# All queries ahead of the attention: four heads packed per weight tile, kept in DRAM

## The chip, the core and the metric

The kernel runs on one core of a Trainium2 chip. The metric is the time of one execution on the device, in microseconds (us); of the kernel before, three timed runs gave 2964.47, 2965.61 and 2966.31. TensorE (PE) multiplies, VectorE (DVE) and ScalarE (ACT) read its results out of PSUM banks and work on tiles in SBUF, GpSimd (POOL) does a few copies, and SyncE (SP) issues nearly all transfers (DMAs).

## The reference, cut to what matters

The kernel computes one step of a two-layer decoder trunk for 1024 prompt tokens and 32 sample tokens (8 sequences of 4). The change lies in the second layer's mixer. Its queries and their use:

```python
def dilated_mixer(h, w_q, q_norm, w_o, pos, attend):
    B, L, _ = h.shape
    q = (h @ w_q).reshape(B, L, N_GROUPS, N_KV, Q_PER_KV, HEAD_DIM)   # 3 x 4 x 2 x 128
    q = rope_partial(rms_norm(q, q_norm), pos)                        # per head; rotary on 32 of 128
    outs, lses = [], []
    for g, (win, dil) in enumerate(DIL_GROUPS):                       # (128,1), (512,4), (2048,16)
        o, l = attend(q[:, :, g], win, dil)
        ...
    w = jax.nn.softmax(jnp.stack(lses), axis=0)
    o = jnp.sum(w[..., None] * jnp.stack(outs), axis=0)
    return o.reshape(B, L, N_QH_GROUP * HEAD_DIM).astype(h.dtype) @ w_o
```

Here `h` is the normalised residual stream (1024 wide). There are 24 query heads of 128: 8 slots (4 key/value heads times 2), each with three dilations. The prompt's attention runs over windows of 128 keys in classes of the token's number (1, 4, 16 steps apart); the sample tokens look into a cache of 1024 older keys and values. Per slot the three results are mixed by their softmax denominators.

## The kernel before, in words

Activations lie transposed: 128 features on the partitions, T = 1056 tokens (1024 prompt, 32 sample) along a row, worked on in three chunks of 352. Every large product is made of three single-pass products: a weight and an activation are each split into a rounded high part and a rest (`whi`/`wlo`, `XH`/`XL`), and `whi*XH + whi*XL + wlo*XH` are summed. A query head needs 8 feature tiles times 3 times 3 chunks = 72 matmuls of 352 columns.

The part that the change touches begins when `shared_kv` has issued its last product, and ends when the FFN that follows begins. It is staged so:

- `shared_kv` makes the four keys and values, writes them to `Kd` and `Vd` in DRAM, and splits the residual into `XH`/`XL`. Of its two wide PSUM pools one is given up ahead of the last value product (`hand_over`), and three one-bank buffers `mq` take its place.
- `Mixer.queries(s)` makes the three heads of slot s, one `wtile` of 512 KB weights each, through `proj` (L937). Each chunk goes through `qk_head`: scaled by the token's `rstd` (L829), squared (L831), split, summed over the 128 features by two matmuls with a matrix of ones into `p_n` (L800, L801), turned into a norm by Ln and Exp (L802, L803), applied (L805; L809 for the dilated heads, which are put into classes on the way), and rotated (L817 to L820; 32 partitions).
- `Mixer.attend(s)` makes the 8 score tiles of the near window (L973) and 8 double tiles of the dilated ones (L984), each taken out by DVE with mask and minimum (L966) and by ACT with Exp (L967). The weights that mix the three results go once through DRAM (`scr`, `scr2`, `cA`). The value half (`dilated`, `near_by`) scales the tiles on DVE, transposes them on PE, copies them on ACT (L1022, L1043), multiplies them with the values into `p_o`, and stores `o` to `Ad`.
- `Mixer.sample(h, half)` runs after every second slot, twice: five cache tiles `kk` (256 KB, two buffers) into `p_ss`, a softmax, five tiles `vv` into `p_os`.
- After slot 7 the first half of the output product (4 of 8 slots) runs through the same `proj`, 288 matmuls on `OH`/`OL`; they too stand at L937.

The program is written in this order (queries of slot s+1 behind the attention of slot s), and a scheduler then sorts each engine's instructions within what the buffers allow: on TensorE, matmuls of the next slot's queries stand between those of the attention. An engine works its list in order; each instruction can wait for others.

Of the kernel before, what the change touches and what calls it, by code (L numbers as in the profile page):

```python
# [8 lines left out]
F32 = mybir.dt.float32  # L9
# [9 lines left out]
NP, NS = 1024, 32  # L19
# [12 lines left out]
QB = 4  # L32
# [3 lines left out]
def yoco_step_kernel(  # L36
# [10 lines left out]
    raw_stack, mma_stack, mmb_stack, mq_stack = (ExitStack() for _ in range(4))  # L47
# [23 lines left out]

    def hand_over():
        mma_stack.close()
        mm.pools.pop(0)
        return psum("mq", mq_stack, bufs=3)

    def close_products():
        raws.pools.pop()
        raw_stack.close()
        mma_stack.close()  # L80
        mmb_stack.close()
# [47 lines left out]
    Vd = dr.tile([T, 512], F32, name="Vd")  # L129

# [85 lines left out]

    def like(t, s, ps):
        return t[:, s] if len(ps.shape) == 2 else t[:, s].rearrange("p (c n) -> p c n", c=3)
# [9 lines left out]
    def norm_done(ssq, n=D):  # L228
# [564 lines left out]
    def qk_head(chunks, g, tab, tp, dst, pre, late, classes=False, early=False):  # L793
# [4 lines left out]
        def finish(s, q, t, th, tl):  # L798
# [5 lines left out]
            if not classes:  # L804
                nc.vector.scalar_tensor_tensor(dst[:, s], q, g, t, op0=ALU.mult, op1=ALU.mult)  # L805
                return
            e = min(s.stop, NP) - s.start
            u = slice(s.start // 4, (s.start + e) // 4)
            nc.vector.scalar_tensor_tensor(  # L809
                dst[:, :NP].rearrange("p (r u) -> p u r", r=4)[:, u], q[:, :e].rearrange("p (u r) -> p u r", r=4), g,  # L810
                t[:, :e].rearrange("p (u r) -> p u r", r=4), op0=ALU.mult, op1=ALU.mult)
            if e < CW:
                nc.vector.scalar_tensor_tensor(dst[:, NP:], q[:, e:], g, t[:, e:], op0=ALU.mult, op1=ALU.mult)
# [29 lines left out]
    def shared_kv(X, ssq, tp):  # L843
        with tc.tile_pool(name="kvp", bufs=1) as kvp:
# [4 lines left out]
            norm_done(ssq)  # L849
# [29 lines left out]
        return mq  # L879

    def to_class(ap):
        return ap.rearrange("p (u r) -> p r u", r=4)

    class Mixer:
        def __init__(self, st, mq):
            def pool(name, bufs, **k):
                return st.enter_context(tc.tile_pool(name=name, bufs=bufs, **k))

            self.mq = mq
            self.po = sm.pools[1]
            self.sc = pool("sc", 2, space=PSUM, side="right")
            self.tr = pool("tr", 1, space=PSUM, side="right")
            p = self.pool = pool("mx", 1)
            self.mask_a = p.tile([128, 256], F32, name="mask_a")
            self.mask_b = p.tile([128, 768], F32, name="mask_b")
            self.mask_s = p.tile([128, 656], F32, name="mask_s")
            self.Qs = [p.tile([128, 8, 32], F32, name=f"Qs{h}") for h in range(4)]
            self.kn = p.tile([128, 4, 32], F32, name="kn")  # L900
            self.os = p.tile([128, 8, 8, 4], F32, name="os")
            self.tab = [rope_table(p, i) for i in range(2)]
            self.head(0)
            self.pre = ln_exp_set()
            for h in range(4):
                nc.gpsimd.memset(self.Qs[h], 0.0)

        def loads(self):
# [3 lines left out]
            for h in range(4):  # L912
                nc.sync.dma_start(self.kn[:, h], Kd[h][:, NP:])

        def head(self, h):

            cols = slice(h * 128, (h + 1) * 128)
# [419 lines left out]
```

## Time and profile before

| | us |
|---|---|
| timed runs, median of 3 | 2965.61 |
| profiled execution | 2967.59 |
| its span | 2965.8 |
| TensorE busy | 2909.5 (98%) |
| VectorE busy | 1845.1 (62%) |
| ScalarE busy | 1085.1 (37%) |
| the mixer, first query matmul to first FFN matmul | 1473.3 to 2069.0 |

The span is what the profile covers of the profiled execution; 1.8 us lie outside it. Busy time counts matmuls whose ends are modelled, so a busy TensorE is not one at its peak. The stretch of the change is a fifth of the span; the rest of the kernel is the same in both.

### The profile page before, as it was taken

To read this page: it belongs to the slowest core of one execution; us is meant where nothing else is said; L and a number is where in the kernel's file an instruction comes from. 1 tells how busy PE (TensorE), PEld (TensorE's weight loads), DVE (VectorE), ACT (ScalarE), POOL (GpSimd) and SP (SyncE) were. 2 spreads that over 40 slices of the span, in tenths; PEclk is the share of its full clock that TensorE was granted. 3 is DMA by queue.
4 is the path that set the end of the run, shared out by engine and by line. 5 is a ranking of instruction groups with operands and counts; after the bars stand their busy time and mean duration, and the time that the engine had idled before them with its cause. 6 is when DMAs were issued, how large, how long until landed. Compare 5 with 4: busy or idle time off the path is not lost.

```text
span 2965.8 us, 47230 instructions
## 1 busy us (share of the span) xinstructions
PE 2909.5 (98%) x19920; PEld 2762.0 (93%) x19920; DVE 1845.1 (62%) x2769; ACT 1085.1 (37%) x1761; POOL 19.9 (1%) x44
## 2 busy tenths in 40 slices
PE   8999999999999999999999999999999999999999
PEld 7889898899999999999988879788899999999999
DVE  6345455776766544467687778784676666654364
ACT  5233333522222221235455555552532222231141
POOL 0000000000000000000000000000000000000000
PEclk9999999999999999999999999999999999999999
DMA  3121234322222442132433141334422222262123
GB/s 129 59 74 51 74 140 142 119 80 80 81 72 87 171 129 74 41 127 102 132 91 107 59 122 44 115 107 134 167 79 73 87 72 80 76 237 75 50 77 110
DMA packets 133987, 291.06 MB, mean 98 GB/s; under 512 B 34160, under 2 KB 58736, under 8 KB 132752
## 3 DMA queue, kind: packets, MB, share of 16 engines
q1 hardware_dynamic: 133040, 287.72, 29.4%
q8 instruction: 157, 2.57, 0.4%
q14 instruction: 54, 0.44, 0.1%
q10 hardware_dynamic: 736, 0.33, 0.0%
HBM read 216.14 MB, written 71.86 MB: 97 GB/s over the span
## 4 chain that ended last, share of the span: by engine, by line
PE 88%; DVE 6%; DMA 3%; ACT 2%; issue 1%; SPq 0%; DVEq 0%; ACTq 0%
PE mm L271 38%; PE be L207 13%; PE ga L207 9%; PE al L207 8%; PE mm L937 6%; PE mm L671 2%; PE p_s L984 1%; PE p_o L1052 1%; PE mm L289 1%; DMA vv<-in_cv_dram 1%; DMA kk<-in_ck_dram 1%; DVE hs L817 1%; DVE q L809 1%; PE p_s L973 1%; DVE q L819 1%
## 5 line engine op out<-in xcount | busy, mean ns | idle before, releaser
L134 ACT CAST whi<-raw 128x1024 fp32r<-128x1024 f32 (+2 forms) x244 | 197.6, 810 | 789.3 <-PE mm L271 578.5
L135 DVE TENSOR_TENSOR wlo<-raw,whi 128x1024 fp32r<-128x1024 f32 (+2 forms) x244 | 224.6, 921 | 80.0 <-ACT whi L134 79.9
L764 DVE TENSOR_TENSOR X<-mm,X 128x1056 f32<-128x1056 f32 (+1 forms) x100 | 121.1, 1213 | 235.7 <-PE mm L271 235.5
L271 PE MATMUL mm<-XH,wlo 128*128 128x352 f32 x1104 | 245.3, 328 | 4.7 <-DVE wlo L135 4.7
L271 PE MATMUL mm<-XH,whi 128*128 128x352 f32 x1104 | 249.3, 331 | 0.2 <-ACT q_in L295 0.2
L271 PE MATMUL mm<-XL,whi 128*128 128x352 f32 x1104 | 247.3, 328 | 0.2 <-DVE XL L138 0.2
L134 ACT CAST hw<-S 128x512 fp32r<-128x512 f32 x176 | 108.8, 621 | 314.7 <-PE ga L207 181.8
L271 PE MATMUL mm<-GH,wlo 128*128 128x352 f32 x1038 | 223.6, 324 | 0.0
L271 PE MATMUL mm<-GL,whi 128*128 128x352 f32 x1038 | 223.6, 323 | 0.0
L271 PE MATMUL mm<-GH,whi 128*128 128x352 f32 x1038 | 223.3, 323 | 0.0
L207 PE MATMUL be<-Bh,hw 128*128 128x264 f32 x1056 | 216.6, 286 | 5.2 <-ACT hw L134 5.2
L207 PE MATMUL be<-Bl,hw 128*128 128x264 f32 x1056 | 215.8, 286 | 0.0
L207 PE MATMUL be<-Bh,lw 128*128 128x264 f32 x1056 | 214.9, 285 | 0.0
L271 PEld LDWEIGHTS mm<-XH,wlo 128*128 128x128 f32 x1104 | 189.0, 190 | 8.0 <-DVE wlo L135 5.3
L271 PEld LDWEIGHTS mm<-XH,whi 128*128 128x128 f32 x1104 | 188.6, 189 | 8.2 <-issue 3.1
L271 PEld LDWEIGHTS mm<-XL,whi 128*128 128x128 f32 x1104 | 190.2, 189 | 4.1 <-issue 1.3
L937 PE MATMUL mm<-XL,whi 128*128 128x352 f32 x576 | 193.7, 336 | 0.0
L937 PE MATMUL mm<-XH,whi 128*128 128x352 f32 x576 | 193.7, 336 | 0.0
L937 PE MATMUL mm<-XH,wlo 128*128 128x352 f32 x576 | 189.3, 329 | 0.0
L271 PEld LDWEIGHTS mm<-GL,whi 128*128 128x128 f32 x1038 | 177.0, 188 | 0.3 <-DVE GL L135 0.2
L271 PEld LDWEIGHTS mm<-GH,whi 128*128 128x128 f32 x1038 | 176.6, 188 | 0.0
L271 PEld LDWEIGHTS mm<-GH,wlo 128*128 128x128 f32 x1038 | 176.5, 189 | 0.0
(342 smaller groups left out, 6292.9 us busy)
## 6 DMA issues: line engine op xcount, KB each, us to landing
raw<-in_w_fi_dram SPq DMA_DIRECT2D x88, 512.0 KB, 3.5
Gd<-g SPq DMA_DIRECT2D x44, 528.0 KB, 2.7
gr<-Gd SPq DMA_DIRECT2D x44, 528.0 KB, 4.9
raw<-in_w_fo_dram SPq DMA_DIRECT2D x64, 256.0 KB, 2.7
raw<-in_w_a_dram SPq DMA_DIRECT2D x24, 512.0 KB, 3.5
raw<-in_w_q_dram SPq DMA_DIRECT2D x24, 512.0 KB, 3.7
kk<-in_ck_dram SPq DMA_DIRECT2D x40, 256.0 KB, 3.5
vv<-in_cv_dram SPq DMA_DIRECT2D x40, 256.0 KB, 2.9
```

Of the source, the lines that this page charges most:

```text
L134: nc.scalar.copy(hi, x)
L135: nc.vector.tensor_tensor(lo, x, hi.bitcast(F32), op=ALU.subtract)
L207: nc.tensor.matmul(ps[:, c, :HC], a[:, k, :], b[:, c * HC:(c + 1) * HC], start=(first and k == 0 and i == 0), stop=(k == len(xs) - 1 and i ...
L271: nc.tensor.matmul(ps[:, c, :CW], a[:, k, :], b[k][:, c * CW:(c + 1) * CW], start=(k == 0 and i == 0), stop=(k == n - 1 and i == 2),)
L289: nc.tensor.matmul(ps, a[:, k, :], b[k][:, s], start=(k == 0 and i == 0), stop=(k == n - 1 and i == 2))
L671: nc.tensor.matmul(ps[:, c, :CW], raw[:, 128 * k:128 * k + 128], ps_[k][:, c * CW:(c + 1) * CW], start=(k == 0), stop=(k == 1))
L764: nc.vector.tensor_tensor(like(X[m], s, p), p, like(X[m], s, p), op=ALU.add)
L809: nc.vector.scalar_tensor_tensor(dst[:, :NP].rearrange("p (r u) -> p u r", r=4)[:, u], q[:, :e].rearrange("p (u r) -> p u r", r=4), g, t[: ...
L817: nc.vector.stream_shuffle(t[32:64], dst[:32], [(a + 16) % 32 for a in range(32)])
L819: nc.vector.tensor_tensor(dst[:32], dst[:32], tab[:32], op=ALU.mult)
L937: nc.tensor.matmul(ps, a[:, k, :], b[k][:, s], start=(k == 0 and i == 0), stop=(k == n - 1 and i == 2))
L973: nc.tensor.matmul(ps[:, :n], q[0][:, j * 128:(j + 1) * 128], self.KA[:, k0:k0 + n], start=True, stop=True)
```

## The change

A new function `queries()` makes all 24 heads before any attention. It works through six groups (a dilation g and four of the eight slots, t4). A group loads four heads' weights (4 x 512 KB) into one tile `RR` and makes four products, each packing 32 features of four heads, with the wide PSUM pools of `shared_kv` kept for them. The four squares are summed in `S`, one pair of matmuls per chunk with a block matrix of ones (`block_r`) gives all four heads' norms, the rotary part (now 128 partitions of the first product) is done once per group, and the token's `rstd` is not applied, since the head norm divides it out: only its small constant is kept (`Ed`, from `norm_done`). `finish` multiplies and writes 16 pieces of 32 partitions to `Qd` in DRAM. It runs one product late, behind the first product of the next group in the program's text.

The attention then reads `Qd` (`load`, four buffers). `attend` is cut in two: `scores(s+1)` is issued ahead of `values_out(s)`, with twice the `pA` and `pB` buffers; the transposes use two PSUM banks in turn.

```diff
@@ norm_done(ssq, n=D, eps=None)
+            if eps is not None:
+                nc.vector.tensor_scalar(eps[:, s], p, 128 * EPS / n, 128 * EPS * EPS, op0=ALU.mult, op1=ALU.add)
...
@@ shared_kv
-            norm_done(ssq)
+            eps = tp.tile([128, T], F32, tag="s", name="eps", bufs=4)
+            norm_done(ssq, eps=eps)
+            nc.sync.dma_start(Ed, eps)
...
-                if h == 3:
-                    mq = hand_over()
...

+    def queries():
+        with tc.tile_pool(name="qp", bufs=1) as qp:
+            E = qp.tile([128, T], F32, name="E")
+            gq = qp.tile([128, 4], F32, name="gq")
+            heads = [slice(32 * a, 32 * a + 32) for a in range(4)]
+            for a in heads:
+                for b in range(4):
+                    nc.scalar.dma_start(gq[a, b:b + 1], gains[heads[b], G_Q:G_Q + 1])
+            nc.sync.dma_start(E, Ed)
+            zo = qp.tile([128, 128], F32, name="zo")
+            nc.gpsimd.memset(zo, 0.0)
+            for a in heads:
+                nc.gpsimd.memset(zo[a, a], 1.0)
+            block_r = qp.tile([128, 128], F32R, name="block_r")
+            nc.vector.tensor_copy(block_r, zo)
+            pre = ln_exp_set()
+            def qt(name, tag, bufs=1, dtype=F32):
+                return qp.tile([128, T], dtype, tag=tag, name=name, bufs=bufs)
+            def put(g, out, x, f):
+                if g == 0:
+                    f(v3(out), x)
+                    return
+                for c in range(3):
+                    e = min(CW, NP - c * CW)
+                    u = slice(c * CW // 4, (c * CW + e) // 4)
+                    f(by_class(out[:, :NP])[:, :, u], to_class(x[:, c, :e]))
+                    if e < CW:
+                        f(out[:, NP:], x[:, c, e:])
+            def finish(g, t4, hb, S):
+                th, tl, t = qt("th", "th", dtype=F32R), qt("tl", "tl", dtype=F32R), qt("t", "t")
+                split(th, tl, S)
+                for c in range(3):
+                    s = slice(c * CW, (c + 1) * CW)
+                    p = sm.tile([128, CW], F32, tag="sm", name="p_n")
+                    nc.tensor.matmul(p, block_r, th[:, s], start=True, stop=False)
+                    nc.tensor.matmul(p, block_r, tl[:, s], start=False, stop=True)
+                    nc.vector.tensor_tensor(t[:, s], p, E[:, s], op=ALU.add)
+                nc.scalar.activation(t, t, AF.Ln, scale=1.0 / 128)
+                if g:
+                    nc.scalar.activation(by_class(S[:, :NP]), to_class(t[:, :NP]), AF.Exp, scale=-0.5)
+                    nc.scalar.activation(S[:, NP:], t[:, NP:], AF.Exp, scale=-0.5)
+                else:
+                    nc.scalar.activation(S, t, AF.Exp, scale=-0.5)
+                for b in range(4):
+                    nc.vector.tensor_tensor(hb[b], hb[b], S, op=ALU.mult)
+                    for a in range(4):
+                        nc.sync.dma_start(Qd[3 * (4 * t4 + a) + g][heads[b]], hb[b][heads[a]])
+            late = None
+            table = None
+            for g, t4 in ((0, 0), (1, 0), (2, 0), (1, 1), (2, 1), (0, 1)):
+                if table != (g > 0):
+                    table = g > 0
+                    cos, sin = qt("cos", "cos"), qt("sin", "sin")
+                    for a in heads:
+                        nc.sync.dma_start(cos[a], c_rope[int(table)][0:32])
+                        nc.sync.dma_start(sin[a], c_rope[int(table)][32:64])
+                RR = qp.tile([128, 4, 8, 128], F32, tag="RR", name="RR")
+                for a in range(4):
+                    nc.sync.dma_start(RR[:, a].rearrange("p k m -> p (k m)"), w_q[3 * (4 * t4 + a) + g])
+                hb = []
+                for b in range(4):
+                    hi, lo = (wp.tile([128, 8, 128], F32R, tag=t, name=t) for t in ("whi", "wlo"))
+                    split(*(t[:].rearrange("p k (a c) -> p a k c", a=4) for t in (hi, lo)), RR[:, :, :, heads[b]])
+                    ps = proj((hi, lo), XH, XL)
+                    h = qt("hb", "hb", 6)
+                    if b == 0:
+                        S = qt("S", "S")
+                        with tc.issue_after(pre.ins):
+                            nc.scalar.activation(v3(S), ps, AF.Square)
+                    else:
+                        q = qt("sq", "sq")
+                        nc.scalar.activation(v3(q), ps, AF.Square)
+                        nc.vector.tensor_tensor(S, S, q, op=ALU.add)
+                    put(g, h, ps, lambda o, i: nc.scalar.activation(o, i, AF.Copy, scale=gq[:, b:b + 1]))
+                    if b == 0:
+                        x = qt("hs", "hs")
+                        nc.vector.stream_shuffle(x, h, [(a + 16) % 32 for a in range(32)])
+                        nc.vector.tensor_tensor(x, x, sin, op=ALU.mult)
+                        nc.vector.tensor_tensor(h, h, cos, op=ALU.mult)
+                        nc.vector.tensor_tensor(h, h, x, op=ALU.add)
+                        if late:
+                            finish(*late)
+                    hb.append(h)
+                late = g, t4, hb, S
+            finish(*late)
...

@@ Mixer
+        def load(self, s):
+            q = [self.a.tile([128, T], F32, tag="q", name="q", bufs=4) for _ in range(3)]
+            for g in range(3):
+                nc.sync.dma_start(q[g], Qd[3 * s + g])
...
-                t = pool.tile([128, 256], F32, tag="pA", name="pA", bufs=8)
+                t = pool.tile([128, 256], F32, tag="pA", name="pA", bufs=16)
...
-                    t = pool.tile([128, 2 * n], F32, tag=f"pB{h}", name="pB", bufs=4)
+                    t = pool.tile([128, 2 * n], F32, tag=f"pB{h}", name="pB", bufs=8)
...
-                p = tr.tile([128, 3, 128], F32, tag="tr", name="p_t")
+                p = tr.tile([128, 3, 128], F32, tag="sm" if tr.n % 2 else "tr", name="p_t")
...
@@ mixer
-            mx = Mixer(st, mq)
-            q = mx.queries(0)
-            mx.loads()
+            mx = Mixer(st)
+            queries()
+            xh_stack.close()
+            close_banks()
+            mx.start()
+            now = mx.scores(mx.load(0))
             for s in range(8):
-                if s and s % 2 == 0:
-                    mx.head(s // 2)
-                mx.attend(s, q)
+                after = None
+                if s < 7:
+                    if s % 2:
+                        mx.keys(s // 2 + 1)
+                    after = mx.scores(mx.load(s + 1))
+                mx.values_out(s, *now)
                 if s % 2:
+                    if s < 7:
+                        mx.values(s // 2 + 1)
                     for half in range(2):
                         mx.sample(s // 2, half)
-                if s < 7:
-                    q = mx.queries(s + 1)
-            xh_stack.close()
+                now = after
```

Three places of the new order matter. The first is SyncE's list behind the last value head, `rows` being that head's values turned to rows. Before:


```order
L874 DMA Vd<-rows 128x8x128
L875 DMA Vd<-rows 32x128
L874 DMA out_dram<-rows 128x8x128
L875 DMA out_dram<-rows 32x128
L260 DMA raw<-in_w_q_dram 128x1024
L839 DMA tab_13252<-in_c_rope_dram 64x1056
L839 DMA tab_13254<-in_c_rope_dram 64x1056
L919 DMA KA<-Kd_157 128x1024
```

And after; behind these rows stand three more pairs of `cos` and `sin` and then the four loads of `RR`:

```order
L872 DMA out_dram<-rows 128x8x128
L873 DMA out_dram<-rows 32x128
L984 DMA mask_a<-in_c_mask_a_dram 128x256
L985 DMA mask_b<-in_c_mask_b_dram 128x768
L986 DMA mask_s<-in_c_mask_s_dram 128x656
L988 DMA kn<-Kd_157 128x32
L988 DMA kn<-Kd_158 128x32
L988 DMA kn<-Kd_159 128x32
L988 DMA kn<-Kd_160 128x32
L1005 DMA KA<-Kd_157 128x1024
L889 DMA E<-Ed 128x1056
L940 DMA cos<-in_c_rope_dram 32x1056
```

The query weight that stood directly behind the last value rows is gone, as are two others among the earlier heads' rows; the first packed weights stand behind seventeen other loads.

The second place is TensorE's list where one set of norms is formed (`p_n`). Before, within a slot's queries, with what each row waits for:

```order
L937 MATMUL mm<-XL_13211,whi 128x352
L801 MATMUL p_n<-htl,ones_r 128x352 [waits DVE_49]
L937 MATMUL mm<-XH_13203,wlo 128x352
L937 MATMUL mm<-XH_13204,whi 128x352
L937 MATMUL mm<-XL_13212,whi 128x352
L937 MATMUL mm<-XH_13204,wlo 128x352
L937 MATMUL mm<-XH_13197,whi 128x352
L800 MATMUL p_n<-hth,ones_r 128x352 [waits Activation_49]
L801 MATMUL p_n<-htl,ones_r 128x352 [waits DVE_49]
L937 MATMUL mm<-XL_13205,whi 128x352
```

After, at the end of the second group (the next begins with `mm<-XH_13223,whi`); the ends of the fourth and fifth read alike, those of the first and third have their `p_n` one product later:

```order
L278 MATMUL mm<-XL_13238,whi 128x352 x3
L278 MATMUL mm<-XH_13230,wlo 128x352 x3
L919 MATMUL p_n<-th,block_r 128x352 [waits Activation_49]
L919 MATMUL p_n<-th,block_r 128x352
L920 MATMUL p_n<-tl,block_r 128x352 [waits DVE_49]
L920 MATMUL p_n<-tl,block_r 128x352
L919 MATMUL p_n<-th,block_r 128x352 [waits DVE_49]
L920 MATMUL p_n<-tl,block_r 128x352
L278 MATMUL mm<-XH_13223,whi 128x352 [waits PE_49,Activation_49]
L278 MATMUL mm<-XH_13223,whi 128x352 x2
L278 MATMUL mm<-XL_13231,whi 128x352 x3
```

The matmuls of the norm stood between query matmuls, and now stand behind the group's last product and ahead of the next group's first.

The third place is TensorE's list at a sample half, where `kk` is the cache of keys. Before:

```order
L937 MATMUL mm<-XH_13199,whi 128x352
L937 MATMUL mm<-XL_13207,whi 128x352
L1083 MATMUL p_ss<-kk,Qs_13246 32x128 [waits DMAHW3_49]
L1083 MATMUL p_ss<-kk,Qs_13246 32x128 x3
L937 MATMUL mm<-XH_13199,wlo 128x352
L937 MATMUL mm<-XH_13200,whi 128x352
L937 MATMUL mm<-XL_13208,whi 128x352
L1083 MATMUL p_ss<-kk,Qs_13246 32x128 [waits DMAHW4_49]
L1083 MATMUL p_ss<-kk,Qs_13246 32x128 x3
L937 MATMUL mm<-XH_13200,wlo 128x352
L937 MATMUL mm<-XH_13201,whi 128x352
```

And after, with the transposes (`p_ts`) of the same half behind it:

```order
L1167 MATMUL p_ss<-kk,Qs_13265 32x128 [waits DMAHW2_49]
L1167 MATMUL p_ss<-kk,Qs_13265 32x128 x3
L1167 MATMUL p_ss<-kk,Qs_13265 32x128 [waits DMAHW6_49]
L1167 MATMUL p_ss<-kk,Qs_13265 32x128 x3
L1170 MATMUL p_ss<-kn,Qs_13265 32x16 x4
L1167 MATMUL p_ss<-kk,Qs_13265 32x128 [waits DMAHW7_49,DVE_49]
L1167 MATMUL p_ss<-kk,Qs_13265 32x128 x3
L1167 MATMUL p_ss<-kk,Qs_13265 32x128 [waits DMAHW0_49]
L1167 MATMUL p_ss<-kk,Qs_13265 32x128 x3
L1167 MATMUL p_ss<-kk,Qs_13265 32x128 [waits DMAHW1_49]
L1167 MATMUL p_ss<-kk,Qs_13265 32x128 x3
L1199 MATMUL p_ts<-ident,es 128x128 [waits DVE_49]
```

Between the cache tiles stood query matmuls, which wait for no transfer; now one cache tile's matmuls follow the other's.

## Rows read from the trace of the kernel before

**Rows 1.** The page: busy time and share of each engine

```profile
PE 2909.5 (98%) x19920; PEld 2762.0 (93%) x19920; DVE 1845.1 (62%) x2769; ACT 1085.1 (37%) x1761; POOL 19.9 (1%) x44
```

**Rows 2.** Stretches of the mixer: start:end, length, busy time of each engine, granted clock, DMA

```profile
1473.30:1976.60 503.30, 484.40 (x3308) 432.27 (x3308) 387.97 (x938) 272.00 (x652) 15.81 (x30) 1.00 0.29 85
1976.60:2069.00 92.40, 84.29 (x610) 71.57 (x609) 55.96 (x153) 36.46 (x81) 1.39 (x2) 0.96 0.56 175
1516.00:1651.00 135.00, 129.39 (x903) 114.37 (x904) 103.35 (x263) 71.98 (x179) 4.08 (x7) 0.99 0.29 83
```

**Rows 3.** Query products: minimum, median, maximum ns; first and last start

```profile
L937 PEld LDWEIGHTS mm<-XH,whi x576: 186/188/289, 1473.3 to 1976.0; 128*128 128x128 f32 x192
```

**Rows 4.** The chain that ended last, one pair of slots: start, length, what

```profile
1516.08 1.13 PE p_s L973 x4
...
1530.56 1.31 PE p_s L984 x8
1532.67 1.31 PE p_s L984 x8
...
1540.16 4.71 DMA scr<-stW
1544.88 2.27 DMA cA<-scr
...
1556.90 3.87 PE mm L937 x24
```

**Rows 5.** The same chain, the fourth pair

```profile
1919.16 0.98 PE p_s L973 x4
```

**Rows 6.** The same chain, the last slot and the output product

```profile
1989.38 2.72 PE mm L937 x8
...
2008.40 4.39 DMA kk<-in_ck_dram
...
2013.24 0.48 PE p_t L1020 x3
...
2021.97 1.98 PE p_o L1052 x16
...
2045.49 23.54 PE mm L937 x146
2069.03 3.07 PE mm L271 x19
```

**Rows 7.** SyncE's queue behind the last value head

```profile
1478.76 1.12 SPq L874 DMA_DIRECT2D out_dram<-rows  x1
...
1480.68 1.04 SPq L260 DMA_DIRECT2D raw<-in_w_q_dram  x1
1483.61 1.14 SPq L839 DMA_DIRECT2D tab<-in_c_rope_dram  x2
```

**Rows 8.** The chain at that place, and the stretch behind it

```profile
1479.93 3.56 DMA out_dram<-rows
...
1483.50:1493.50 10.00, 8.92 (x52) 8.10 (x52) 6.85 (x10) 6.16 (x12) 3.23 (x5) 1.00 1.03 281
```

**Rows 9.** ScalarE and VectorE on whole rows of 1056, and a strided copy

```profile
1473.17 1.18 ACT L137 ACTIVATE XH<-X,gt 128x1056 fp32r<-128x1056 f32 x1 [0.27 <-PE mm L271]
...
1475.66 1.06 ACT L134 CAST whi<-raw 128x1024 fp32r<-128x1024 f32 x1
...
1474.17 1.25 DVE L298 TENSOR_TENSOR vh<-mm,rstd 128x1056 f32<-128x1056 f32 x1
...
L1030 ACT COPY o<-p_o 128x512 f32<-128x512 f32 x4 | 4.3, 1082 | 0.5 <-PE p_o L1028 0.4
```

**Rows 10.** The granted clock around a wait of TensorE

```profile
1986.00:1988.00 2.00, 0.73 (x3) 0.45 (x3) 1.99 (x2) 0.70 (x1) 0.00 (x0) 1.00 1.10 144
...
1990.00:1992.00 2.00, 2.00 (x9) 2.00 (x8) 1.66 (x2) 0.00 (x0) 1.18 (x1) 0.50 0.69 201
2010.00:2020.00 10.00, 8.91 (x67) 6.73 (x67) 4.19 (x20) 5.26 (x10) 0.00 (x0) 1.00 0.43 105
```

More of the change, by code (lines that the diff above doesn't have):

```diff
@@ L31 @@
 EP_AT = (3, 5, 6)
-QB = 4
 @with_exitstack
@@ L46, in yoco_step_kernel @@
     xh_stack = ExitStack()
-    raw_stack, mma_stack, mmb_stack, mq_stack = (ExitStack() for _ in range(4))
+    raw_stack, mma_stack, mmb_stack = (ExitStack() for _ in range(3))
     def psum(name, stack=ctx, **k):
@@ L129, in yoco_step_kernel @@
     Vd = dr.tile([T, 512], F32, name="Vd")
+    Qd = [dr.tile([128, T], F32, name=f"Qd{k}") for k in range(24)]
+    Ed = dr.tile([128, T], F32, name="Ed")
     def split(hi, lo, x, g=None):
@@ L803, in finish @@
             nc.scalar.activation(t, t, AF.Exp, scale=-0.5)
[L804 to L813, printed above, removed]
+            nc.vector.scalar_tensor_tensor(dst[:, s], q, g, t, op0=ALU.mult, op1=ALU.mult)
         def rotate():
@@ new lines, in yoco_step_kernel, with __init__ @@
+    class Mixer:
+        def __init__(self, st):
+            self.st = st
+            a = self.a = self.open("mxa")
+            self.mask_a = a.tile([128, 256], F32, name="mask_a")
+            self.mask_b = a.tile([128, 768], F32, name="mask_b")
+            self.mask_s = a.tile([128, 656], F32, name="mask_s")
+            self.Qs = [a.tile([128, 8, 32], F32, name=f"Qs{h}") for h in range(4)]
+            self.kn = a.tile([128, 4, 32], F32, name="kn")
+            self.os = a.tile([128, 8, 8, 4], F32, name="os")
@@ L913, in loads, with open, start, keys @@
                 nc.sync.dma_start(self.kn[:, h], Kd[h][:, NP:])
-        def head(self, h):
+            self.keys(0)
+        def open(self, name, bufs=1, **k):
+            return self.st.enter_context(tc.tile_pool(name=name, bufs=bufs, **k))
+        def start(self):
+            self.mq = self.open("mq", 3, space=PSUM)
+            self.po = sm.pools[1]
+            self.sc = self.open("sc", 2, space=PSUM, side="right")
+            self.tr = Turns(sm.pools[0], self.open("tr", 1, space=PSUM, side="right"))
+            self.pool = self.open("mx")
+            self.values(0)
+        def keys(self, h):
+            self.KA = self.a.tile([128, NP], F32, tag="KA", name="KA")
+            nc.sync.dma_start(self.KA, Kd[h][:, :NP])
+            self.KB = self.a.tile([128, NP], F32, tag="KB", name="KB")
+            nc.gpsimd.tensor_copy(by_class(self.KB[:]), to_class(self.KA[:]))
+        def values(self, h):
             cols = slice(h * 128, (h + 1) * 128)
-            self.KA = self.pool.tile([128, NP], F32, tag="KA", name="KA")
-            nc.sync.dma_start(self.KA, Kd[h][:, :NP])
-            self.KB = self.pool.tile([128, NP], F32, tag="KB", name="KB")
-            nc.gpsimd.tensor_copy(self.KB[:].rearrange("p (r u) -> p r u", r=4), to_class(self.KA[:]))
             self.VB = self.pool.tile([128, 8, 128], F32, tag="VB", name="VB")
@@ L938, in proj, with scores @@
                 yield c, ps
[L940 to L943 removed]
+        def load(self, s):
+            q = [self.a.tile([128, T], F32, tag="q", name="q", bufs=4) for _ in range(3)]
+            for g in range(3):
+                nc.sync.dma_start(q[g], Qd[3 * s + g])
                 nc.gpsimd.tensor_copy(
                     self.Qs[s // 2][:, :, g * 8 + s % 2 * 4:g * 8 + s % 2 * 4 + 4],
[L946 to L958 removed]
+                    q[g][:, NP:].rearrange("p (b t) -> p b t", t=4))
+            return q
+        def scores(self, q):
+            pool, sc = self.pool, self.sc
             stA = pool.tile([128, 8, 2], F32, tag="stA", name="stA", bufs=2)
@@ L1191, in yoco_step_kernel @@
     sb.close()
-    mq = shared_kv(X, ssq, tp)
+    shared_kv(X, ssq, tp)
     sx.close()
-    close_products()
-    xp, op, X = mixer(mq)
+    close_raw()
+    xp, op, X = mixer()
     bg2 = sx.enter_context(tc.tile_pool(name="bg2", bufs=20, side="right"))
```

69 lines of the change are left out of this document (19 added, 50 removed).

## The prediction

> **What bounds the kernel now.** I read the page first: TensorE is busy 98% of the span, VectorE 62%, ScalarE 37% [rows 1]. A change that takes work from VectorE and ScalarE alone gains nothing while that holds, so the question is whether it holds in the mixer. The windows say yes for its first 503.3 us: TensorE works 484.4 of them at a granted clock of 1.00, and only 18.9 us are idle; in a pair of slots it works 129.4 of 135 us while VectorE works 103.4 [rows 2]. Only the last 92.4 us, where the queries have run out, are looser, at a granted clock of 0.96 [rows 2]. The chain of waits then shows what a query costs: 24 of its matmuls in 3.87 us, 0.161 us each [rows 4], so a head of 72 takes 11.6 us and the 24 heads (576 times three matmuls, [rows 3]) 278.2 us. The whole mixer, from the first query weights at 1473.3 [rows 3] to the first FFN matmul at 2069.0 [rows 6], takes 595.7 us. This is the stretch that I forecast; the rest is the same code.
>
> The first pair of slots begins at 1516.08 and the fourth at 1919.16 [rows 4, 5], so a pair takes 134.4 us. Of that, six heads are 69.6, and their 36 norm matmuls, as wide, are 5.8. So 59.0 us a pair is what attention and samples cost TensorE today, with their waits filled by query matmuls. That number decides the case, since the change takes the filler away.
>
> **The change, part by part.**
>
> *Query products.* Packing four heads' quarters changes which columns stand in a weight tile, not their number: 24 products of 72 matmuls stay, 278.2 us. The norm's matmuls fall from 144 to 36: 5.8 us, a gain of 17.4.
>
> *VectorE and ScalarE work.* Scaling by rstd goes, as do 24 separate rotations; they lay beside the products, in 103.4 of 135 us [rows 2]. Worth nothing on the path.
>
> *Start.* The packed weights come behind seventeen other loads in SyncE's queue, and the first of these waits until the value rows have landed (the pools reuse memory). Before, a query weight was issued at 1480.68 and the tables at 1483.61 [rows 7], right as the rows' transfer ended (1479.93 + 3.56 = 1483.49, [rows 8]); TensorE had two weights already loaded and stayed 8.92 of 10 us busy [rows 8]. Now nothing is at hand. The loads are 0.84 MB of masks, 0.06 of new keys, 0.52 of `KA`, 0.54 of `E`, 1.08 of tables and 2.1 of weights, 5.1 MB; at the 281 GB/s of that stretch [rows 8] 18.3 us, so 1501.8. The rounded weights take another 1.06 [rows 9]: TensorE starts near 1502.9, 29.6 us after 1473.3, of which the transposes of the last value head fill one: 28. If the transfers run at twice that speed it is 20, if SyncE's issues are the limit 34. Behind such an idle stretch the clock falls: the granted clock was 0.50 soon after a stretch with 0.73 of 2 us at work, and eight matmuls took 2.72 us where 1.29 were due [rows 6, 10]. I add 3 us, seen as a stretch of some 6 us at half speed. Together **31**.
>
> *Group ends.* For the second, fourth and fifth group the order has the norm's matmuls directly behind the group's fourth product and ahead of the next first one. TensorE then waits for the fourth product's square (1.18) and its store in classes on ScalarE, which is strided (1.08 for 512 columns, so 2.2 for 1056), the rounded sum (1.1) and its rest on VectorE (1.25), all from [rows 9], then six matmuls of 0.161 and one addition between banks (0.5): 7.3 us, three times, **22**. Below, nothing, if the sum is faster than the store; above, 30. The first and third groups have a product between, which hides it.
>
> *Hand-over.* The first attention tile reuses the memory of the query buffers, so it waits until the last sixteen pieces have landed. Behind the last product: square, addition, rounding and rest (4.7), norms (1.5), Ln and Exp (2.4), four multiplications (5.0) from [rows 9], four issues behind the last (1.6) and a landing (3.6, as [rows 8]): 18.8, and a first score tile, **20** (14 to 26). Nothing stands on TensorE's list there but six score matmuls.
>
> *Attention alone.* The order interleaves scores of a slot with values of the one before, so the round trip through `scr` is covered; but the sample's cache tiles now stand one behind the other, and each wait for `kk` (4.39 us, [rows 6]) is TensorE's own. The lower bound: sixteen score tiles at 2.11 us for four ([rows 4], 1530.56 to 1532.67) are 8.4, and the last slot's values took 10.7 from first transpose to last product ([rows 6], 2013.24 to 2023.95). A slot is 19.1, a pair 38.2, with about 6 for the two sample halves 44. The upper one: nothing is gained or lost against today, 59.0, and with cold matmuls more. Without filler the engines wait for each other at each tile (two score banks, VectorE's list in order), yet those waits are partly in the 59.0 already. I take 59.0, the measured one: four pairs less the 9 of the last pair's samples, which fall into the output product, 227, and 4 for matmuls at the lower clock, **231**.
>
> *Output product.* From the last `p_o` (2021.97 + 1.98) to the FFN took 45.1 us [rows 6] with 231 of the 288 matmuls; now 240 stand there: **46**.
>
> Sum: 31 + 278 + 6 + 22 + 20 + 231 + 46 = 634 us against 595.7, 38.3 more. The profiled execution would be 2967.6 + 38.3 = 3005.9 (span 2965.8, 1.8 outside); on the median of the runs, 2965.6 + 38.3 = **3004**.
>
> **A rule against the change.** The trace shows TensorE's clock at 0.50 after a wait that left it 0.73 of 2 us busy, and at 1.00 where it was busy 8.91 of 10 with small matmuls [rows 10]. The Trainium skill ("TensorE: Matmul & The Clock Gate", section "Loop structure matters more than you think") says that matmuls which follow one another keep the array at speed, while a loop that waits for a transfer ahead of its matmuls runs at the lower clock throughout. By that rule the sample blocks would pull the whole attention down; this case's rows bear it out at 1990 and speak against it at 2010. It is the second rival.
>
> **The rivals.**
>
> *1. Faster: the attention packs.* With no query matmul in between, scores and values run at the lower bound, 44 a pair: 4 x 44 - 6 = 170 instead of 231, 573 in all: 2943. For it: VectorE and ScalarE have far less to do, and the round trip is covered. Against it: `kk` waits, two score banks, and 71 us of new idle time that must first be paid. The point of decision: 192 us for the attention, 50 a pair.
>
> *2. Slower: the attention runs at half clock.* A matmul cost 2.72 / 8 = 0.34 at 0.50 against 0.161 [rows 6], 2.1 times. Most of the 44 us a pair are TensorE's; doubled, 80 a pair, 4 x 80 - 11 = 309, 78 more than the forecast: 3082. Decided by whether the waits at score and sample tiles come often enough to keep the clock down.
>
> *3. The start is covered:* if the pools let the weights load while the value rows are still written, the gap shrinks to 10 and the time to 2983. The list of SyncE speaks against it.
>
> *4. The change doesn't do what it says:* if scores and values don't overlap on the chip, a slot pays the round trip through DRAM (4.71 + 2.27 = 7 us, [rows 4]) and the pair is 73: 4 x 14 = 56 more, 3060. TensorE's list has them mixed, so this goes with rival 2.
>
> **How the numbers follow.** Forecast 0.55 (2985 to 3025); rival 1 0.17; rivals 2 and 4 0.16; rival 3 0.12. A measurement of this kernel can tell about 0.2%, 6 us, from no change. Rival 1 gives faster 0.17; no difference lies between it and rival 3, and takes 0.06 from the low ends of rival 3 and the forecast; the rest, 0.77, is slower. The range must leave out 0.2 at most: below 2950 lies most of rival 1, above 3065 most of rival 2, so **2950 to 3065**.
>
> **What would show it.** In the profile after: TensorE idle from about 1476 to 1503 with the weights' transfer as releaser; 24 products of 11.6 us; three gaps of 7 us in front of `p_n`; 20 us without matmuls behind the last product; then four pairs of 59 us at a granted clock of 0.9 or more, and 46 us of output product. Wrong it would be if a pair takes under 50 us, if the clock of the attention is near 0.5, or if the start gap is missing.

## The result

The changed kernel takes 3050.39 us (median of four runs, 3047.67 to 3053.27) against 2965.04 of the kernel before in the same session: a ratio of 1.0289 (95% interval 1.0271 to 1.0307), 85 us slower. The forecast was 3004, 38 us slower, with a range of 2950 to 3065. The sign and most of the mechanism held, the size did not: 47 us more than forecast were lost, 39 of them in one term of the sum.

The page of the changed kernel, its busy times (before: [rows 1]):

```profile
PE 2906.4 (95%) x19812; PEld 2763.3 (91%) x19812; DVE 1712.2 (56%) x2517; ACT 1035.2 (34%) x1591; POOL 18.5 (1%) x49
```

VectorE lost 133 us of work and ScalarE 50, and the kernel became slower: TensorE's work stayed (2906 against 2909 us) and its idle time grew. The windows, cut at the stages of the forecast; the columns are those of [rows 2]:

```profile
1472.50:1504.70 32.20, 1.64 (x12) 0.97 (x10) 3.45 (x5) 4.61 (x7) 3.67 (x10) 0.55 0.66 194
1504.70:1816.10 311.40, 297.29 (x1760) 292.68 (x1761) 116.79 (x112) 97.92 (x138) 1.21 (x4) 0.95 0.27 84
1816.10:1837.50 21.40, 3.16 (x11) 1.56 (x9) 9.80 (x13) 5.40 (x6) 0.00 (x0) 0.61 0.85 274
1837.50:2107.90 270.40, 217.50 (x1664) 168.57 (x1668) 158.52 (x660) 141.77 (x397) 10.84 (x23) 0.90 0.58 158
2107.90:2155.10 47.20, 47.16 (x369) 42.28 (x369) 22.15 (x48) 10.39 (x18) 0.00 (x0) 1.00 0.53 171
```

They are the start without weights, the six groups of products, the hand-over, the attention, and the output product up to the FFN's first matmul. Together 682.6 us, where before 595.7 lay between the same points (1473.3 to 2069.0, [rows 3, 6]); the last value product ended 0.8 us earlier. Beside the forecast:

| stage | forecast | measured |
|---|---|---|
| start, with the lower clock behind it | 31 | 32.2, and 2.5 for the first 18 matmuls |
| products, norms, group ends | 278 + 6 + 22 = 306 | 308.9 |
| hand-over | 20 | 21.4 |
| attention | 231 | 270.4 |
| output product | 46 | 47.2 |
| sum | 634 | 682.6 |

Four stages are right within 4 us. The attention is 39 us too long. What TensorE waited for there, and what it waited for in the pairs of slots before (first group: changed kernel, 1837.5 to 2108; second: kernel before, 1516 to 1976; total us, times, longest):

```profile
PE p_ss L1167 <- DMA kk<-in_ck_dram: 23.7, 13, 3.8
PE p_s L1054 <- DVE stA L1047: 16.5, 2, 14.3
PE p_os L1211 <- DMA vv<-in_cv_dram: 10.1, 7, 2.5
PE p_o L1136 <- ACT o L1114: 4.6, 6, 2.3
```

```profile
PE p_os L1127 <- DMA vv<-in_cv_dram: 5.1, 5, 1.8
PE p_t L1041 <- DVE pA L1038: 3.3, 3, 1.4
PE p_ss L1083 <- DMA kk<-in_ck_dram: 3.0, 4, 0.9
```

The waits for the cache tiles rose from 8.1 to 33.8 us; up to the FFN's first matmul they are 9.5 in the kernel before and still 33.8 in the changed one. (The 14.3 us at `stA` are the end of the hand-over, put down to the attention's first tile.) One sample block in the chain of waits, and the window over it:

```profile
1894.75 5.37 DMA kk<-in_ck_dram
1900.17 0.70 PE p_ss L1167 x8
1900.88 3.97 DMA kk<-in_ck_dram
1904.90 0.66 PE p_ss L1167 x8
1905.63 0.67 PE p_ss L1167 x8
1906.32 2.62 DMA kk<-in_ck_dram
1908.98 0.66 PE p_ss L1167 x8
```

```profile
1898.00:1908.00 10.00, 2.69 (x40) 1.23 (x40) 3.72 (x19) 1.12 (x3) 0.00 (x0) 0.56 0.77 222
1908.00:1918.00 10.00, 8.82 (x91) 5.35 (x92) 4.99 (x28) 4.27 (x16) 0.00 (x0) 0.76 0.60 197
```

A cache tile is four matmuls, and each stands as two instructions in the trace, so x8 is one tile. Two tiles, a wait for the next transfer, two tiles, a wait: TensorE works 2.69 of 10 us, its granted clock is 0.56 there, and 0.76 in the ten that follow, though it is busy again. A tile's eight instructions, which took 0.35 to 0.43 us before, now take 0.66.

### The profile page after: what moved, and what is told of

The parts are those of the page before. It is cut to its first block, busy times and chain, and to the rows that moved or that the text cites. A ratio compares the mean times of both kernels' runs of the same rounds, so it can differ in the third digit from the quotient of the medians.

```text
span 3049.8 us, 46799 instructions
## 1 busy us (share of the span) xinstructions
PE 2906.4 (95%) x19812; PEld 2763.3 (91%) x19812; DVE 1712.2 (56%) x2517; ACT 1035.2 (34%) x1591; POOL 18.5 (1%) x49
## 4 chain that ended last, share of the span: by engine, by line
PE 89%; DMA 4%; DVE 3%; ACT 2%; issue 1%; SPq 0%; ACTq 0%; DVEq 0%
PE mm L278 46%; PE be L204 13%; PE ga L204 8%; PE al L204 8%; PE mm L678 2%; PE mm L1026 2%; DMA kk<-in_ck_dram 1%; DMA vv<-in_cv_dram 1%; PE p_s L1054 1%; PE mm L296 1%; PE p_o L1136 1%; PE p_s L1065 1%; PE p_u L506 1%; PE p_us L524 1%; PE p_o L515 1%
## 5 line engine op out<-in xcount | busy, mean ns | idle before, releaser
L131 ACT CAST whi<-raw 128x512 fp32r<-128x512 f32 (+2 forms) x220 | 172.5, 784 | 775.9 <-PE mm L278 582.9
L278 PE MATMUL mm<-XH,whi 128*128 128x352 f32 x1680 | 376.6, 330 | 29.6 <-ACT whi L131 28.3
L278 PE MATMUL mm<-XL,whi 128*128 128x352 f32 x1680 | 373.9, 328 | 0.0
L278 PEld LDWEIGHTS mm<-XH,whi 128*128 128x128 f32 x1680 | 289.3, 191 | 38.3 <-ACT whi L131 30.4
L278 PEld LDWEIGHTS mm<-XH,wlo 128*128 128x128 f32 x1680 | 288.9, 191 | 8.4 <-DVE wlo L132 5.7
L278 PEld LDWEIGHTS mm<-XL,whi 128*128 128x128 f32 x1680 | 291.5, 191 | 3.7 <-issue 1.9
L132 DVE TENSOR_TENSOR wlo<-raw,whi 128x512 fp32r<-128x512 f32 (+2 forms) x220 | 195.5, 888 | 92.2 <-ACT whi L131 92.2
L204 PEld LDWEIGHTS be<-Bh,hw 128*128 128x128 f32 x1056 | 163.9, 189 | 5.6 <-ACT hw L131 5.4
L204 PEld LDWEIGHTS be<-Bl,hw 128*128 128x128 f32 x1056 | 164.6, 189 | 0.0
L204 PEld LDWEIGHTS be<-Bh,lw 128*128 128x128 f32 x1056 | 163.6, 188 | 0.1
```

The source lines that it names most:

```text
L131: nc.scalar.copy(hi, x)
L132: nc.vector.tensor_tensor(lo, x, hi.bitcast(F32), op=ALU.subtract)
L204: nc.tensor.matmul(ps[:, c, :HC], a[:, k, :], b[:, c * HC:(c + 1) * HC], start=(first and k == 0 and i == 0), stop=(k == len(xs) - 1 and i ...
L278: nc.tensor.matmul(ps[:, c, :CW], a[:, k, :], b[k][:, c * CW:(c + 1) * CW], start=(k == 0 and i == 0), stop=(k == n - 1 and i == 2),)
```

## The experiments

The theory after the result: the attention lost the query matmuls as cover for the sample blocks' cache transfers, and pays the waits and the lower clock behind them. The rival: with two score banks and in-order engines, score and value tiles wait for each other, samples or not. Each kernel was timed beside runs of the kernel before on the same chip, whose medians lie between 2961.7 and 2965.3.

**Cache tiles ahead.**

```diff
-                kk = sp.tile([128, 512], F32, tag="kk", name="kk", bufs=2)
+                kk = self.kp.tile([128, 512], F32, tag="kk", name="kk", bufs=8)
...
-                vv = sp.tile([128, 512], F32, tag="vv", name="vv", bufs=2)
+                vv = self.kp.tile([128, 512], F32, tag="vv", name="vv", bufs=8)
```

`kp` is a pool that lies where the activations were, and is closed ahead of the output product's loads.

> Eight buffers each for the cache tiles kk and vv instead of two, so their transfers are issued well ahead; nothing else changed. Theory (the attention without query matmuls waits for the cache tiles and then runs its matmuls at the lower clock): the 33.8 us that TensorE waited for kk and vv in the changed kernel's attention fall to under 10, and some 10 to 15 us of lower clock go with them: 3005 to 3020 us. Rival (the engines wait for each other at every score and value tile, and the cache waits only stand where another wait would be): the waits turn up at score tiles on VectorE and ScalarE, 3040 or more.

Measured: 3013.23 us (ratio 1.0167, 1.0151 to 1.0183), 37 less than the changed kernel, as the theory had it. The attention and the output product in its windows:

```profile
1839.30:2063.80 224.50, 195.79 (x1688) 159.39 (x1692) 153.19 (x659) 140.53 (x396) 11.21 (x23) 0.95 0.62 178
2063.80:2116.70 52.90, 49.65 (x351) 48.10 (x341) 23.52 (x50) 11.09 (x19) 0.00 (x0) 0.97 0.59 200
```

No wait for `kk` or `vv` is left. The attention is 45.9 us shorter and the output product 5.7 longer, but these two windows don't hold the same work: of the output product's 288 matmuls, 48 stand in the attention of the changed kernel and 16 here. The two stages together hold 2028 matmul instructions in both (the changed kernel first):

```profile
1837.50:2155.10 317.60, 264.66 (x2028) 210.86 (x2029) 180.67 (x708) 152.16 (x415) 10.84 (x23) 0.91 0.57 160
1839.30:2116.70 277.40, 245.44 (x2028) 207.49 (x2029) 176.71 (x708) 151.62 (x415) 11.21 (x23) 0.95 0.62 182
```

They became 40.2 us shorter, and their 277.4 are the forecast's 231 + 46. Of the 40.2 us, 21.0 are idle time of TensorE (52.9 to 32.0) and 19.2 are shorter work for the same matmuls, at a clock that went from 0.91 to 0.95. A new wait appears, 15.0 us for the samples' softmax:

```profile
PE p_ts L1199 <- DVE es L1195: 15.0, 3, 5.6
```

**First weights ahead.**

```diff
+        for a in range(4):
+            nc.sync.dma_start(raw[:].rearrange("p (k a c) -> p k a c", k=8, a=4)[:, :, a],
+                              w_q[3 * a].rearrange("p (k m) -> p k m", k=8)[:, :, 32 * b:32 * b + 32])
...
     shared_kv(X, ssq, tp)
+    first.extend(first_tile(b) for b in range(2))
     sx.close()
```

> The first group's weights are loaded in packed form straight into the two raw weight buffers while the value heads are still made, in runs of 128 bytes; the other five groups as in the changed kernel. Theory (the idle 28.3 us at the start are the weights' late place behind the value rows): the gap at the start falls to under 3 us, the lower clock behind it too, 3017 to 3024 us. Rival (the transfers of short runs and the seventeen loads in front only move the gap to the third product): 3035 or more, with a wait of 10 us or more for the third product's weights.

Measured: 3017.02 us (1.0183, 1.0166 to 1.02), 33 less, at the lower end of the theory's range. In the window 1473 to 1500 TensorE now works 24.7 of 27 us:

```profile
1473.00:1500.00 27.00, 24.70 (x155) 23.96 (x153) 7.11 (x8) 8.65 (x10) 3.72 (x10) 1.00 0.68 175
```

The gap is gone but for 4.9 us ahead of the third product. From 1473 on, up to the last query product, 26 us are won; the rest of the 33 comes behind it (see the three together). That kernel's DMA issues of the same time (KB each, us to landing) show that the packed transfers, 1024 runs of 128 bytes each, land in 3.8 us:

```profile
raw<-in_w_q_dram SPq DMA_DIRECT2D x12, 128.0 KB, 3.8
```

**Norms one product later.**

```diff
...
-                        if late:
-                            finish(*late)
+                    if b == 1 and late:
+                        finish(*late)
```

> The norms of a group are formed behind the second product of the next group in the program's text (two buffers for S; hs shares a buffer with sq), so that no p_n stands directly behind a group's last product but at the end of all. Theory (the stalls at three group ends cost what TensorE waits there, some 9 us, and some 6 us of lower clock behind them): 3033 to 3039 us. Rival (the forecast's 22 us): 3026 to 3030. Third possibility: query buffers now come free later and ScalarE waits for the pieces in DRAM, then 3045 or more.

Measured: 3037.26 us (1.0248, 1.0231 to 1.0265), 13 less, in the theory's range, but only in part for its reason. In the changed kernel the second, fourth and fifth group end alike; here the second (start, us, and the wait before it):

```profile
1600.96 0.65 PE L278 MATMUL mm<-XH,wlo 128*128 128x352 f32 x3
1605.19 0.60 PE L919 MATMUL p_n<-th,block_r 128*128 128x352 f32 x2 [3.58 <-ACT th L131]
...
1608.51 1.08 PE L278 MATMUL mm<-XH,whi 128*128 128x352 f32 x3
```

From the last product's end to the next product's first matmul are 6.9 us, three times, as the forecast had it with 7.3. TensorE waits 13.2 us of them at `p_n`, and behind each gap three matmuls take 0.88 us instead of 0.48 for a while, some 6 us in all (granted clock 0.50 from 1608.5 to 1612). With the edit the first two gaps are gone, and the one behind the fifth group is longer:

```profile
1744.37 0.65 PE L278 MATMUL mm<-XH,wlo 128*128 128x352 f32 x3
1748.60 0.95 PE L919 MATMUL p_n<-th,block_r 128*128 128x352 f32 x2 [3.59 <-ACT th L131]
...
1756.95 1.25 PE L278 MATMUL mm<-XH,whi 128*128 128x352 f32 x3 [4.83 <-ACT whi L131]
1758.00 1.08 PE L278 MATMUL mm<-XL,whi 128*128 128x352 f32 x3
1761.95 1.25 PE L278 MATMUL mm<-XH,wlo 128*128 128x352 f32 x3 [2.87 <-DVE wlo L132]
```

There the norm still stands directly behind the group's last product, and the next weights are rounded behind the norm's work on ScalarE and VectorE: 11.9 us without products, and 2.9 more six matmuls later. So the stage is only 6 us shorter, and the rest of the 13 comes behind the last query product.

**The three together.**

> The three edits together: cache tiles ahead, first weights ahead, norms one product later. If the three losses are independent the gains add: by the theory 31 + 15 + 38, so about 2966 us, level with the kernel before (2950 to 2980). By the rival for the cache tiles 2995 to 3010. In both cases the hand-over of some 20 us and the attention without filler remain.

Measured: 2980.65 us (1.0059, 1.0044 to 1.0074), 70 less than the changed kernel and 16 slower than before; just above what was expected. The single gains add to 84. The 14 us between are found behind the last query product: from its last matmul to the output product's last the changed kernel takes 339.3 us (1815.8 to 2155.1), the first weights ahead 331.7 and the norms' edit 331.0. So 8 us of each single gain were not at the start or the group ends at all, but came from the attention, which the edit doesn't touch. Its waits for `kk` and `vv` are 31.3 and 29.1 us there instead of 33.8, which is 2.5 and 4.7 of the 8. With the cache tiles ahead there is nothing of that kind left to win: 299.4 alone, 303.6 with all three, in an execution of 2984.72 us.

**Without the samples, changed and before.**

```diff
                     for half in range(2):
-                        mx.sample(s // 2, half)
...
```

Zeros are stored for the sample tokens' attention, in both.

> The changed kernel without the sample tokens' attention (no kk, vv, p_ss, p_os; zeros are stored in its place), all else as changed. Theory (what the attention lost with the query matmuls is cover for the sample blocks' cache transfers): the samples cost 85 to 105 us here, so 2945 to 2965, and a pair of slots takes about 45 us at a granted clock near 1.0. Rival (score and value tiles wait for each other, samples or not): the samples cost no more than their own work and waits between them, 40 to 60 us, 2990 to 3010, and a pair still takes 57 or more.

> The kernel before without the sample tokens' attention, zeros stored in its place. Theory: among query matmuls the samples cost little more than their own matmuls, 8 times 4 to 5 us, 2925 to 2935. Rival: they cost about as much as in the changed kernel, under 2915.

Measured: 2948.25 us and 2905.93 us. The samples cost 102 us in the changed kernel and 58 in the one before (2964.39 in that session): 44 more, which is the 47 that the forecast missed but for 3. Without samples the change costs 42 us, near the 38 of the forecast. In the kernel before they cost more than I expected (58 against some 36), so the second expectation failed; the time that its rival gave, under 2915, was met, but not its reason, since 58 is far from 102. The scores and values alone cost the same with and without query matmuls around: in the changed kernel from the first score tile at 1835.6 to the last value product at 2010.4, 43.7 us a pair, at a clock of 1.00 once they run:

```profile
1878.00:1958.00 80.00, 74.58 (x488) 64.79 (x487) 65.35 (x271) 58.86 (x175) 6.84 (x14) 1.00 0.56 151
```

In the kernel before, a pair without samples takes 118.4 us (1515.0 to 1633.4), less 75.4 for its queries and norms 43.0. So the rival falls: tiles that wait for each other are no part of the loss, and scores and values take what they took before, 43.7 against 43.0.

**Values ahead of the next scores.**

```diff
...
-                    after = mx.scores(mx.load(s + 1))
                 mx.values_out(s, *now)
...
+                    now = mx.scores(mx.load(s + 1))
```

> The changed kernel with each slot's values in front of the next slot's scores, as in the kernel before; all else as changed. Theory (without other matmuls the round trip of the mixing weights through DRAM, some 7 to 10 us a slot, is only covered by the next slot's scores): 45 to 80 us slower than the changed kernel, 3095 to 3130. Rival (the scheduler brings scores forward anyway, or the sample blocks cover it): 3040 to 3065.

Measured: 3068.54 us (1.0353, 1.0339 to 1.0368), 18 slower than the changed kernel; below the theory's range, 3.5 above the rival's. The slot that scores run ahead is worth 18 us, not the whole round trip eight times: TensorE waits 11.1 us for the scaled `pB` tiles, while the waits for `kk` fall from 23.7 to 9.1 and those for `vv` rise from 10.1 to 12.2. That part of one wait is hidden behind the other is argued from these lists, not shown.

**Work put into the waits.**

```diff
+                for _ in range(4):
+                    nc.tensor.matmul(out, ident, self.mask_s[:, :128], start=True, stop=True)
                 for q, b, rs in quads():
```

> The changed kernel with four more matmuls of 128 columns (a constant, overwritten by the real scores) ahead of each cache tile's matmuls: 160 in all, some 18 us of TensorE work at 0.11 us each, two fifths of them or more in the 24 us that it waits for kk anyway. Theory A (the lower clock behind the cache waits costs 10 us or more of the attention by itself): the granted clock of the attention rises from 0.90 to over 0.95 and the time falls to 3030 to 3045 though work was added. Theory B (the waits themselves are the cost, the lower clock next to nothing): the clock may rise, but the time stays or grows, 3050 to 3062.

Measured: 3070.27 us (1.0354, 1.0337 to 1.0371), 20 slower, more than either expectation. The added work was twice what I had put: the 160 matmuls stand as 320 in the trace. Each is 275 ns long there, but they overlap, and at full clock they follow each other at 0.11 us (eight transposes of 128 columns took 0.87 in this kernel's chain): 35 us. The group, the wait, and the window of attention and output product:

```profile
L1167 PE MATMUL p_ss<-mask_s,ident x320: 275/275/583, 1889.9 to 2128.0; 128*128 128x128 f32 x160
```

```profile
PE p_ss L1169 <- DMA kk<-in_ck_dram: 7.2, 5, 2.9
```

```profile
1837.90:2175.20 337.30, 302.82 (x2348) 247.29 (x2349) 180.01 (x708) 152.01 (x415) 10.54 (x23) 0.95 0.54 150
```

The wait for `kk` falls by 16.5 us and the clock of the two stages rises from 0.91 to 0.95, but they take 337.3 us instead of 317.6. Idle time is 18.5 us less, busy time 38.2 more: more than the 35, since a part of the added matmuls runs at the lower clock itself (one group of eight in 2.01 us, at a granted clock of 0.50). So neither theory's number held and filling the waits with empty work doesn't pay here. How the 40 us of the cache tiles split between waiting and clock is not settled by this run; it rests on the busy times above.

**Three tries at the rest.** From the three edits on, I tried to win what is left: the hand-over, and the wait for the samples' softmax. First all at once: score tiles in memory that comes free with the last query matmul, masks and `KA` loaded behind the first group, one sample half behind each slot:

```diff
-                    for half in range(2):
-                        mx.sample(s // 2, half)
+                mx.sample(s // 2, s % 2)
...
-                t = pool.tile([128, 256], F32, tag="pA", name="pA", bufs=16)
+                t = self.sp.tile([128, 256], F32, tag="pA", name="pA", bufs=16)
```

> The three edits of the first call and three more: the score tiles stand in their own memory that comes free with the last query matmul and not with the last piece in DRAM; masks, new keys and KA are loaded behind the first group; one sample half follows each slot instead of two every second slot. Theory: of the 2981 us of the three edits the hand-over gives 12 to 16, the third product's weights 5 to 8, and the waits for the sample's softmax 10 to 20, so 2940 to 2955, 10 to 25 faster than the kernel before. Rival (without query matmuls the attention can't fill TensorE whatever is moved): 2965 to 2980, because each wait that is removed comes back at the next tile.

Measured: 2985.9 us (1.0075, 1.0062 to 1.0087), no gain on the three edits' 2980.65, and above both expectations. The 14 us wait at the first score tile is gone, and these stand in TensorE's list of waits instead (1465 to 2130):

```profile
PE p_s L1087 <- DVE stB L1069: 12.3, 5, 6.0
PE p_s L1076 <- DVE sts L1199: 9.9, 5, 3.4
PE p_o L1133 <- ACT o L1136: 8.5, 8, 2.4
```

Then the parts apart:

> The cache tiles ahead as in the first experiment, and one sample half behind each slot instead of two behind every second; nothing else. It tells which of the three further edits of the version before gave nothing. Theory (the score tiles' place on the right made the output product's first tiles wait for the attention's end and set the last norms among the first scores): the spreading alone saves the 10 to 15 us that TensorE waits for the samples' softmax, 2995 to 3005. Rival (a sample half behind each slot only moves that wait to the score tiles): 3008 to 3020.

> The three edits of the first call, with masks and KA loaded behind the first group and one sample half behind each slot, and the score tiles in the place they had in the changed kernel. Theory: 2981 less 5 at the start and less 10 to 15 at the samples, 2960 to 2967, level with the kernel before. Rival (waits that are removed in the attention come back at the next tile): 2975 to 2985.

Measured: 3016.71 us (1.0183, 1.0169 to 1.0197) for the spread halves with cache tiles ahead, against 3013.23 without spreading; 2984.59 (1.007, 1.0057 to 1.0084) with the three edits. In the first of the two, the 15.0 us for the softmax have fallen to 0.9, but TensorE waits 9.8 us for it at score tiles, and the waits at value tiles grow from 5.4 to 11.8: the rival holds. Last, the first head's samples put into the hand-over (with six buffers for the cache tiles):

```diff
+            for half in range(2):
+                mx.sample(0, half)
             now = mx.scores(mx.load(0))
```

> The three edits of the first call, masks and KA behind the first group, and the first head's two sample halves placed between the last query product and the first score tile, where TensorE otherwise waits some 20 us for the last pieces to land; their tiles lie where the activations were. Theory (a sample half is cheap only where its waits meet work that doesn't depend on it, and the hand-over is such a place): 12 to 18 us less than the three edits, 2962 to 2970, level with the kernel before. Rival (the halves delay the last norms, and so the hand-over, by as much as they take): 2977 to 2987.

Measured: 2979.87 us (1.0063, 1.0051 to 1.0075), again no gain, in the rival's range. The chain shows why:

```profile
1787.51 5.11 DMA kk<-in_ck_dram
1792.66 0.65 PE p_ss L1189 x8
...
1807.17 5.72 DMA kk<-in_ck_dram
1812.94 0.70 PE p_ss L1189 x8
...
1814.42 6.03 PE p_s L1076 x16
```

The sample blocks wait for their own transfers there, and the scores begin at 1814.4 instead of 1803.8. No version beat the kernel before.

## Why the prediction missed in size

- **What bounds the kernel.** Right: VectorE and ScalarE gave up 183 us of work and it was worth nothing on the path.
- **Query products and norms.** Right, 24 products of 11.6 us and a shorter norm.
- **Start.** Right: 32.2 us and 2.5 of lower clock against 31. The experiment that loads the first weights earlier gave 26 us back up to the last query product, with 4.9 us of waiting left at the third product.
- **Group ends.** Right: three gaps of 6.9 us against 7.3. The sum had no term for the lower clock behind them, some 6 us; the stage took 308.9 against 306.
- **Hand-over and output product.** Right, 21.4 against 20 and 47.2 against 46.
- **Attention.** Wrong. The failed step is the choice of 59.0 us a pair, with the reason that the engines' waits "are partly in the 59.0 already". By the run without samples the 59.0 hold 43.0 for scores and values and 16.0 for two sample halves, and those 16.0 were measured with query matmuls in every wait for `kk`. The text named that wait, and said that it becomes TensorE's own, and gave it no price: 4 us were added for the clock and none for the wait. It measured 33.8 us for `kk` and `vv`, against 8.1 before, and the matmuls behind the waits run at a lower clock. With the cache tiles ahead the attention and the output product measure 277.4 together, the forecast's 231 + 46, so 59.0 a pair would have been right for a kernel whose transfers run ahead.
- **The rivals.** The first (44 a pair) looks like the 43.7 that the attention takes without samples, but that is chance. Its 44 hold 6 us for the samples, and its 8.4 us for a slot's score tiles are the eight double tiles alone: eight instructions in [rows 4] are two of them, and the eight near tiles (1.13 us for two in the same rows, so 4.5) are left out. With them its bound is 53 a pair. The second, half clock throughout, did not come: the granted clock of the attention is 0.90. It falls to 0.56 in a sample block and is back at 1.00 in most of the stretch between two blocks. So the rule of the Trainium skill ("TensorE: Matmul & The Clock Gate", section "Loop structure matters more than you think") holds for the stretch that waits for transfers, and not for the scores and values next to it. The third did not come either: the gap at the start is there. The fourth was excluded by TensorE's list, and the experiment put its price at 18 us in all where I had 56.
- **Range and chances.** The range held the time by luck: it reached so far because of the second rival, and the reason was another.

What stays open: why the attention was 8 us shorter where only the start or the norms were changed. Shorter waits for the cache tiles show 2.5 and 4.7 us of it; why they were shorter, and the rest, no run shows.

## What to carry to other kernels

A cost that was measured beside independent work is the cost with its waits filled: before that work is taken away, list every transfer that the remaining instructions wait for, and price each by its latency and its number of buffers, not by the share that it had. Where a block is moved out of dense matmuls, give its loads enough buffers to be issued a whole block ahead: six more buffers each for two tiles gave 37 of the 85 us back here. And work taken from engines that are not the bound, 183 us of it, did not pay here for the stages in which the bounding engine had nothing to do: the start, the group ends and the hand-over.

## What the runs showed of the hardware

- A wait of a few us costs TensorE twice: where the waits for the cache tiles went, 21.0 us less idle time came with 19.2 us less work for the same 2028 matmul instructions, at a granted clock of 0.95 instead of 0.91.
- A transfer of 128 KB in 1024 runs of 128 bytes landed in 3.8 us, and one of 512 KB in long runs in 3.7 us (a query weight on the page of the kernel before): a quarter of the bytes in the same time. Packing four heads can be left to the transfer for the first group, as the second experiment did; no run shows it for all six.
- A float32 matmul of 128 columns is two instructions in the trace (160 written, 320 recorded), which follow each other at 0.11 us where the clock is full.
